# A merge whose gates take seven products for eight, with one branch's product and the plain projection ahead of them

## Chip, cores, metric

One core of a Trainium2 chip runs the whole program as one launch. The metric is device time in microseconds. The engines are TensorE (PE; its weight loads are PEld), VectorE (DVE), ScalarE (ACT), GpSimd (POOL) and SyncE (SP), which here issues loads. Each has its own queue of instructions and works through it in order.

## The reference, cut to the stretch that matters

One block over 512 rows of width 1024, in fp32. `h` is the normalised input; `w_in` projects it to eight vectors of 1024 (u, v, four for the HGRN branch, and two gates).

```python
h = _layer_norm(x, ln0_g, ln0_b)
u_r, v_r, q_r, f_r, i_r, g_r, ga_r, gb_r = split(h @ w_in + b_in)
vn  = _layer_norm(gelu(v_r), gm_norm_g, gm_norm_b)       # per 128-row block and 128-column group:
y_a = gelu(u_r) * (einsum("gts,bnsgc->bntgc", w, vn) + b_s)
y_b = _hgrn2(q_r, f_r, i_r, g_r, lb, hg_norm_g)
merged = sigmoid(ga_r) * (y_a @ w_a) + sigmoid(gb_r) * (y_b @ w_b)
h1  = _layer_norm(ALPHA * h + merged @ w_o, ln1_g, ln1_b)
hid = silu(h1 @ w_ffn_gate) * (h1 @ w_ffn_up)
out = _layer_norm(ALPHA * h1 + hid @ w_ffn_down + ple, ln2_g, ln2_b)
```

## The kernel before

**Products.** Every operand of a large product is split into a high part of a type that TensorE takes at full rate (fp32r) and a low part, the remainder; a product is three matmuls, high by high, high by low, low by high. `split` (lines 62 to 66) makes the parts: a cast on ScalarE and a subtraction on VectorE. A unit of weights of 128x1024 is loaded by SyncE into one of three "raw" buffers and split into one of five pairs `wh`, `wl`. `gemm_a` (line 85) multiplies a stripe of 256 columns of a weight by all 512 rows: two units, 48 matmuls with 512 columns. `gemm_b` has the rows as the stationary operand.

**Seven for eight.** `strassen` (line 164) forms a product of a 2x2 block matrix of weights and a 2x2 block matrix of activations with seven block products in place of eight. Its order is X Z Y Z2 Y2 W Y3; GpSimd makes two of the sums of weights and two more are transfers that add. `product_a` (line 216) is one block product: 24 matmuls with 256 columns. X, W and Y3 read the blocks "11", "12" and "22" of the activations, the others combinations of them (s1, a6, a7, a3). Before, only the FFN's gate and up have this form: eleven groups (`up`), of which each makes 256 columns of both.

**Order of the stretch.** The HGRN branch goes over four pairs of heads; the last pair's `scores`, `outputs` and `finish` are woven into the projection of v (two halves, lines 717 to 728). `finish(M)` transposes the heads, gates them and splits them into `ybh`, `ybl`, w_b's operand. Then: the norm of v (`norm_v`, four row blocks, each with VectorE, ScalarE and GpSimd, "spread"); u's four products, each with its GELU; behind each of them `mix`, which multiplies the normed v by the 128x128 matrices of w_s, adds b_s, multiplies by u and splits to `yah`, `yal`. The merge follows, four rounds over 256 output columns: gate a, w_a, gate b, w_b, 48 matmuls each, with Sigmoid on ScalarE, two multiplies and an addition on VectorE, and a split. `residual` loads x anew and norms it (ScalarE, then two GpSimd operations). Then w_o, the norm, the PLE gate, and the FFN.

**What sets the order.** Each instruction is written for one engine. A planner takes them in program order as priorities (`high_priority` moves some up), estimates their times, gives each engine a fixed order and places the buffers; a pool that has been closed gives its space to later ones, which wait for the last reader. PSUM has four tiles of two banks each.

Of the kernel before, what the change touches and what calls it, by code (L numbers as in the profile page):

```python
# [14 lines left out]
P = 128  # L15
# [18 lines left out]
def block_kernel(  # L34
# [50 lines left out]
    def gemm_a(ps, w, c0, acth, actl, name):  # L85

        for kh in range(2):
            h, l = unit_a(w, 4 * kh, c0, f"{name}_{kh}")
            for j in range(2):
                cs = slice(j * P, (j + 1) * P)  # L90
                for k in range(4):
                    kk = 4 * kh + k
                    first, last = kk == 0, kk == KT - 1
                    PE.matmul(ps[:, j, :], h[:, k, cs], acth[:, kk, :], start=first, stop=False)  # L94
                    PE.matmul(ps[:, j, :], h[:, k, cs], actl[:, kk, :], start=False, stop=False)  # L95
                    PE.matmul(ps[:, j, :], l[:, k, cs], acth[:, kk, :], start=False, stop=last)  # L96
# [621 lines left out]
    for c in range(2):  # L718
# [5 lines left out]
        for a in range(2):  # L724
# [15 lines left out]
    norm_v(3)  # L740
    hgb_cm.__exit__(None, None, None)

    rpool = ctx.enter_context(tc.tile_pool(name="rpool", bufs=1, side="right"))
    r1 = rpool.tile([P, TT, D], F32, name="r1")
    yapool_cm = tc.tile_pool(name="yapool", bufs=1, side="right")
    yapool = yapool_cm.__enter__()
    yah = yapool.tile([P, NH, T], F32R, name="yah")
    yal = yapool.tile([P, NH, T], F32R, name="yal")
    with tc.tile_pool(name="gm", bufs=1, side="right") as gp:
        bs = load_bc(gp, gm_b_s[0].rearrange("g t -> (g t)"), "bs")  # L750
        def mix(m, ug):
# [6 lines left out]
            mx = gp.tile([P, 2, T], F32, tag="mx", name=f"mx{m}", bufs=2)  # L758
            for a in range(2):
                g = 2 * m + a  # L760
                V.tensor_tensor(out=mx[:, a, :].rearrange("p (n t) -> p n t", t=P),
                                in0=psm[:, a, :].rearrange("p (n t) -> p n t", t=P),
                                in1=bs[:, g * P:(g + 1) * P].unsqueeze(1).broadcast_to([P, TT, P]), op=ALU.add)
            V.tensor_tensor(out=mx, in0=mx, in1=ug, op=ALU.mult)
            split(yah[:, 2 * m:2 * m + 2, :], yal[:, 2 * m:2 * m + 2, :], mx)

        prev = None
        for m in range(NH // 2):
            psu = proj(OU, m, "gu") if m else psu0
            ug = gp.tile([P, 2, T], F32, tag="ug", name=f"ug{m}", bufs=2)  # L770
# [11 lines left out]
    mgh = mgpool.tile([P, KT, T], F32R, name="mgh")  # L782
    mgl = mgpool.tile([P, KT, T], F32R, name="mgl")
    with tc.tile_pool(name="mg", bufs=1) as mp:

        g0a = load_bc(mp, ln0_g, "g0a")
        b0a = load_bc(mp, ln0_b, "b0a")
        S.activation(g0a, g0a, AF.Copy, scale=ALPHA)
        S.activation(b0a, b0a, AF.Copy, scale=ALPHA)
        nmr = mp.tile([P, TT, 1], F32, name="nmr")  # L790
        V.scalar_tensor_tensor(out=nmr, in0=mr0[:, :, 0:1], scalar=-1.0, in1=mr0[:, :, 1:2], op0=ALU.mult, op1=ALU.mult)

        def residual(t):
            r = r1[:, t, :]
            nc.sync.dma_start(r, xv[:, t, :])
            S.activation(r, r, AF.Identity, scale=mr0[:, t, 1:2], bias=nmr[:, t, :])
            G.tensor_tensor(out=r, in0=r, in1=g0a, op=ALU.mult)
            G.tensor_tensor(out=r, in0=r, in1=b0a, op=ALU.add)

        for m in range(KT // 2):  # L800
            residual(m)
            res = []
            for nm, off, w, ah, al in (("a", OGA, wa, yah, yal), ("b", OGB, wb, ybh, ybl)):
                psg = ps_tile(f"ps_mg{nm}{m}")
                gemm_a(psg, win, off + 256 * m, hh, hl, f"g{nm}{m}")
                sg = mp.tile([P, 2, T], F32, tag="sg", name=f"sg{nm}{m}", bufs=3)
                for a in range(2):
                    S.activation(sg[:, a, :], psg[:, a, :], AF.Sigmoid, bias=bcol(off, 2 * m + a))
                psw = ps_tile(f"ps_mw{nm}{m}")
                gemm_a(psw, w, 256 * m, ah, al, f"w{nm}{m}")  # L810
                V.tensor_tensor(out=sg, in0=psw, in1=sg, op=ALU.mult)
                res.append(sg)
            V.tensor_tensor(out=res[0], in0=res[0], in1=res[1], op=ALU.add)
            split(mgh[:, 2 * m:2 * m + 2, :], mgl[:, 2 * m:2 * m + 2, :], res[0])
    ybpool_cm.__exit__(None, None, None)
    hpool_cm.__exit__(None, None, None)
# [8 lines left out]
    with tc.tile_pool(name="l1", bufs=1) as lp:  # L825
# [229 lines left out]
```

## Time and profile before

| | before |
|---|---|
| median of 3 runs | 953.31 us (951.9 to 953.61) |
| profiled execution | 952.23 us, its span 950.5 us |
| TensorE busy in the span | 936.2 us (98%), 5552 matmuls |
| VectorE, ScalarE, GpSimd busy | 62%, 39%, 21% |
| TensorE clock granted | 0.997 on the mean of the span |

A line of the page's groups reads: line, engine, operation, tiles out<-in, shapes, count | busy time, mean ns of one | idle time of the engine before it and what ended most of it. In the timeline a row has its start in the span, its duration, engine, line, operation and tiles. Matmuls overlap: their spacing is read from starts, not from durations.

### The profile page before, as it was taken

The numbers are of one execution on the slowest core, as the hardware profiler recorded it, in microseconds if no ns is written. First come the engines' busy times: TensorE is split into PE (matmuls) and PEld (weight loads), VectorE is DVE, ScalarE is ACT, GpSimd is POOL, SyncE is SP. The second block draws the span as 40 slices with busy tenths as digits, with TensorE's granted clock in tenths as the row PEclk, the third lists the DMA queues.
The fourth block names the chain that finished last, engine by engine and source line by source line (L and its number), as shares of the span: only waits on it lengthen the run. The fifth ranks groups of instructions, "written<-read, shape, count | busy, mean of one in ns | idle before, by whom it ended". The sixth has DMA issues, their size and how long they took to land.

```text
span 950.5 us, 13396 instructions
## 1 busy us (share of the span) xinstructions
PE 936.2 (98%) x5552; PEld 811.2 (85%) x5552; DVE 587.0 (62%) x652; ACT 366.7 (39%) x456; POOL 200.1 (21%) x142
## 2 busy tenths in 40 slices
PE   8999999999999999999999999999999999999996
PEld 6888888888888888888888888899999999988885
DVE  6567944868249655423333278488878888567527
ACT  6544232333334362223222177444444445333211
POOL 2015310505006037000000001444333440000004
PEclk9999999999999999999999999999999999999998
DMA  7543223223322624232224312965676564258302
GB/s 262 172 144 111 68 69 110 67 68 110 120 81 67 222 89 133 89 103 96 89 98 169 111 70 89 267 151 146 167 168 183 137 161 106 88 190 272 114 24 88
DMA packets 85452, 120.46 MB, mean 127 GB/s; under 512 B 3992, under 2 KB 60944, under 8 KB 85392
## 3 DMA queue, kind: packets, MB, share of 16 engines
q1 hardware_dynamic: 80928, 105.93, 34.1%
q0 software_dynamic: 3168, 11.54, 7.2%
q10 hardware_dynamic: 1296, 2.15, 0.6%
q8 instruction: 43, 0.70, 0.3%
q14 instruction: 17, 0.14, 0.0%
HBM read 101.77 MB, written 6.29 MB: 114 GB/s over the span
## 4 chain that ended last, share of the span: by engine, by line
PE 90%; DVE 5%; ACT 1%; POOL 1%; issue 1%; DMA 1%; SPq 0%; DVEq 0%; POOLq 0%; ACTq 0%
PE ps_f_b L228 4%; PE ps_f_b L226 4%; PE ps_f_b L229 4%; PE ps_d L100 4%; PE ps_d L101 4%; PE ps_d L102 4%; PE ps_f_a L229 3%; PE ps_f_a L226 3%; PE ps_f_a L228 3%; PE ps_mwa L95 2%; PE ps_mwa L96 2%; PE ps_mwa L94 2%; PE ps_i L102 2%; PE ps_i L100 2%; PE ps_v L100 2%; PE ps_f L94 2%
## 5 line engine op out<-in xcount | busy, mean ns | idle before, releaser
L253 POOL TENSOR_TENSOR mr<-mr,nhalf 128x1 f32<-128x1 f32 x12 | 9.8, 821 | 335.2 <-DVE mr L252 335.2
L63 ACT CAST wh_f<-raw_f 128x1024 fp32r<-128x1024 f32 x41 | 43.2, 1053 | 86.4 <-PE ps_f_b L228 38.5
L102 PE MATMUL ps_d<-wh_d,hidl 128*128 128x512 f32 x172 | 66.8, 389 | 0.0
L101 PE MATMUL ps_d<-wl_d,hidh 128*128 128x512 f32 x172 | 66.8, 389 | 0.0
L100 PE MATMUL ps_d<-wh_d,hidh 128*128 128x512 f32 x172 | 66.0, 389 | 0.0
L66 DVE TENSOR_TENSOR wl_f<-raw_f,wh_f 128x1024 fp32r<-128x1024 f32 x41 | 51.2, 1248 | 21.4 <-ACT wh_f L63 21.3
L66 DVE TENSOR_TENSOR wl_f_t<-t_f,wh_f_t 128x1024 fp32r<-128x1024 f32 x22 | 55.5, 2521 | 3.2 <-ACT wh_f_t L63 3.0
L185 POOL TENSOR_TENSOR t_f<-raw_f,raw_f 128x1024 f32<-128x1024 f32 x11 | 26.7, 2428 | 125.9 <-DVE wl_f L66 102.3
L63 ACT CAST wh_d<-raw_d 128x1024 fp32r<-128x1024 f32 x22 | 23.1, 1050 | 62.8 <-PE ps_d L102 23.6
L501 POOL TENSOR_TENSOR k<-sgm,lv 128x512 f32<-128x512 f32 x8 | 16.0, 2023 | 121.6 <-DVE lv L553 121.6
L66 DVE TENSOR_TENSOR wl_d<-raw_d,wh_d 128x1024 fp32r<-128x1024 f32 x22 | 26.9, 1221 | 18.7 <-ACT wh_d L63 18.7
L102 PEld LDWEIGHTS ps_d<-wh_d,hidl 128*128 128x128 f32 x172 | 32.3, 188 | 6.7
L100 PEld LDWEIGHTS ps_d<-wh_d,hidh 128*128 128x128 f32 x172 | 32.2, 188 | 6.6
L101 PEld LDWEIGHTS ps_d<-wl_d,hidh 128*128 128x128 f32 x172 | 32.3, 188 | 6.5
L63 ACT CAST wh_f_t<-t_f 128x1024 fp32r<-128x1024 f32 x22 | 23.1, 1051 | 32.8 <-PE ps_f_b L229 18.0
L185 POOL TENSOR_TENSOR t_f<-t_f,raw_f 128x1024 f32<-128x1024 f32 x11 | 35.1, 3189 | 0.9
L66 DVE TENSOR_TENSOR wl_wb<-raw_wb,wh_wb 128x1024 fp32r<-128x1024 f32 x8 | 14.2, 1779 | 25.7 <-ACT wh_wb L63 25.7
L66 DVE TENSOR_TENSOR wl_wa<-raw_wa,wh_wa 128x1024 fp32r<-128x1024 f32 x8 | 9.8, 1225 | 27.7 <-ACT wh_wa L63 27.7
L66 DVE TENSOR_TENSOR wl_wo<-raw_wo,wh_wo 128x1024 fp32r<-128x1024 f32 x8 | 9.8, 1222 | 25.8 <-ACT wh_wo L63 25.8
L940 DVE TENSOR_TENSOR g<-p,ps_f_b 128x512 f32<-128x512 f32 x11 | 7.6, 688 | 28.8 <-PE ps_f_b L229 28.7
L94 PE MATMUL ps_q<-hh,wh_q 128*128 128x512 f32 x64 | 25.2, 394 | 0.0
L94 PE MATMUL ps_mwa<-yah,wh_wa 128*128 128x512 f32 x64 | 25.2, 394 | 0.0
(376 smaller groups left out, 3186.0 us busy)
## 6 DMA issues: line engine op xcount, KB each, us to landing
raw_f<-in_w_ffn_up_dram SPq DMA_DIRECT2D x22, 512.0 KB, 7.6
raw_f<-in_w_ffn_gate_dram SPq DMA_DIRECT2D x22, 512.0 KB, 3.6
raw_d<-in_w_ffn_down_dram SPq DMA_DIRECT2D x22, 512.0 KB, 3.7
raw_f<-raw_f POOLq DMA_DIRECT2D x11, 512.0 KB, 4.9
t_f<-raw_f POOLq DMA_DIRECT2D x11, 512.0 KB, 7.2
raw_i<-in_w_in_dram SPq DMA_DIRECT2D x8, 512.0 KB, 4.3
raw_f<-in_w_in_dram SPq DMA_DIRECT2D x8, 512.0 KB, 3.7
raw_q<-in_w_in_dram SPq DMA_DIRECT2D x8, 512.0 KB, 3.7
```

Of the source, the lines that this page charges most:

```text
L63: S.copy(h, src)
L66: (eng or V).tensor_tensor(out=l, in0=src, in1=h.bitcast(F32), op=ALU.subtract)
L94: PE.matmul(ps[:, j, :], h[:, k, cs], acth[:, kk, :], start=first, stop=False)
L95: PE.matmul(ps[:, j, :], h[:, k, cs], actl[:, kk, :], start=False, stop=False)
L96: PE.matmul(ps[:, j, :], l[:, k, cs], acth[:, kk, :], start=False, stop=last)
L100: PE.matmul(ps, acth[:, kk, ts], h[:, k, :], start=first, stop=False)
L101: PE.matmul(ps, acth[:, kk, ts], l[:, k, :], start=False, stop=False)
L102: PE.matmul(ps, actl[:, kk, ts], h[:, k, :], start=False, stop=last)
L185: G.tensor_tensor(out=d, in0=a, in1=b, op=ALU.add)
L226: PE.matmul(o, h[:, k, cs], ah[:, k, :], start=first and j == 0 and k == 0, stop=False, skip_group_check=True)
L228: PE.matmul(o, h[:, k, cs], al[:, k, :], start=False, stop=False, skip_group_check=True)
L229: PE.matmul(o, l[:, k, cs], ah[:, k, :], start=False, stop=last and j == 1 and k == 3, skip_group_check=True)
```

## The change

- **Order.** After v come `finish(M)`, the norm of v, w_b's four products with a copy of each result to `mgf` in SBUF (ScalarE), the mix of all eight groups behind w_b's second and third product (result and b_s to `yaf`), u's four products (GELU, multiplied into `yaf`), the gates, w_a's four products.
- **Gates.** `group_a` is the FFN's group, taken out of `up` with its evacuation as a parameter. Four groups make 256 columns of both gates each. Sigmoid is applied in halves with the bias; gate a is stored to DRAM (issued from ScalarE) and loaded again in w_a's stage, gate b is multiplied into `mgf`. The blocks "11", "12" and "22" of h are read in place; `combine_h` makes the four combinations within u's first two products (four GpSimd sums of 128x512 a half, subtractions and splits).
- **y_a** is split in two halves, one within the first gate group, one after the last group in space that h held.
- **Norms.** The norm of v and the residual use `normed(..., False)`: two scalar_tensor_tensors on VectorE in place of a spread over three engines. The residuals of two row blocks go into w_a's stage and two into w_o's. r1 takes the buffer of `yaf`.
- **Merge's results** are split into four pairs of tiles (`mgs`), where there was one pair.

```diff
+    def gemm_t(ps, w, c0, act, name):      # gemm_a with the operand given by a function
...
-    def norm_v(t):
+    finish(M)
+    for t in range(TT):
         mr = gv.tile([P, 2], F32, tag="mrv", name=f"mrv{t}", bufs=2)
-        ln_stats(gv, [vn[:, t, 0:512], vn[:, t, 512:1024]], mr, f"v{t}")
-        normed(vn[:, t, :], mr, gmg, gmb, True)
-
-    norm_v(0)
-    psu0 = proj(OU, 0, "gu")
-    norm_v(1)
-    finish(M)
-    norm_v(2)
-    norm_v(3)
+        ln_stats(gvv, [vn[:, t, 0:512], vn[:, t, 512:1024]], mr, f"v{t}")
+        normed(vn[:, t, :], mr, gmg, gmb, False)
...
+        for m in range(KT // 2):
+            psw = ps_tile(f"ps_mwb{m}")
+            gemm_a(psw, wb, 256 * m, ybh, ybl, f"wb{m}")
+            S.copy(mgf[:, 2 * m:2 * m + 2, :], psw)
+            if m == 1:
+                mix(0)
+                mix(1)
+            elif m == 2:
+                mix(2)
+                mix(3)
...
+        def combine_h(i):
+            f = {}
+            for n, ks, t0 in (("21", 0, HT), ("22", 4, HT), ("11", 0, 0), ("12", 4, 0)):
+                at = (slice(None), slice(ks, ks + 4), slice(t0 + i * P, t0 + i * P + P))
+                f[n] = gp.tile([P, 4, P], F32, tag=f"f{n}", name=f"f{n}_{i}")
+                G.tensor_tensor(out=f[n], in0=hh[at].bitcast(F32), in1=hl[at].bitcast(F32), op=ALU.add)
+            f["s1"] = gp.tile([P, 4, P], F32, tag="fs1", name=f"fs1_{i}")
+            lo = slice(i * P, i * P + P)
+            for n, o, x, y in (("s1", "s1", "21", "22"), ("a7", "21", "21", "11"), ("a6", "11", "11", "s1"), ("a3", "12", "12", "11")):
+                V.tensor_tensor(out=f[o], in0=f[x], in1=f[y], op=ALU.subtract)
+                split(hcomb[n][0][:, :, lo], hcomb[n][1][:, :, lo], f[o])
+
+        for m in range(KT // 2):
+            psu = ps_tile(f"ps_u{m}")
+            gemm_a(psu, win, OU + 256 * m, hh, hl, f"u{m}")
+            if m < 2:
+                combine_h(m)
+            ug = up_.tile([P, 2, T], F32, tag="ug", name=f"ug{m}", bufs=2)
             for a in range(2):
                 S.activation(ug[:, a, :], psu[:, a, :], AF.Gelu_apprx_tanh, bias=bcol(OU, 2 * m + a))
+            y = yaf[:, 2 * m:2 * m + 2, :]
+            V.tensor_tensor(out=y, in0=y, in1=ug, op=ALU.mult)
+    with tc.tile_pool(name="gt", bufs=1) as fp:
+        def out_g(m):
+            def out(i, j, o):
+                for a in range(2):
+                    S.activation(o[:, a, :], o[:, a, :], AF.Sigmoid, bias=bcol((OGA, OGB)[j], 2 * m + a))
+                if j == 0:
+                    S.dma_start(ga_dram[:, 2 * m:2 * m + 2, HT * i:HT * i + HT], o)
+                else:
+                    y = mgf[:, 2 * m:2 * m + 2, HT * i:HT * i + HT]
+                    V.tensor_tensor(out=y, in0=y, in1=o, op=ALU.mult)
+            return out
+
+        for m in range(KT // 2):
+            group_a(wx, fp, [(win, OGA + 256 * m), (win, OGB + 256 * m)], hcomb, f"g{m}", out_g(m))
+            if m == 0:
+                split_ya(yas_pool, 0)
...
     with tc.tile_pool(name="mg", bufs=1) as mp:
+        split_ya(mp, 1)
...
         def residual(t):
-            r = r1[:, t, :]
-            nc.sync.dma_start(r, xv[:, t, :])
-            S.activation(r, r, AF.Identity, scale=mr0[:, t, 1:2], bias=nmr[:, t, :])
-            G.tensor_tensor(out=r, in0=r, in1=g0a, op=ALU.mult)
-            G.tensor_tensor(out=r, in0=r, in1=b0a, op=ALU.add)
+            nc.sync.dma_start(r1[:, t, :], xv[:, t, :])
+            normed(r1[:, t, :], mr0[:, t, :], g0a, b0a, False)
 
         for m in range(KT // 2):
-            residual(m)
...
+            ga = mp.tile([P, 2, T], F32, tag="ga", name=f"ga{m}", bufs=2)
+            nc.sync.dma_start(ga, ga_dram[:, 2 * m:2 * m + 2, :])
+            psw = ps_tile(f"ps_mwa{m}")
+            gemm_t(psw, wa, 256 * m, lambda kk: tuple(z[:, kk % 4, :] for z in yas[kk // 4]), f"wa{m}")
+            if m in (1, 2):
+                residual(m - 1)
+            with tc.high_priority(offset=400):
+                V.tensor_tensor(out=ga, in0=psw, in1=ga, op=ALU.mult)
+            o = mgf[:, 2 * m:2 * m + 2, :]
+            V.tensor_tensor(out=o, in0=o, in1=ga, op=ALU.add)
+            mgs.append(tuple(mgpool.tile([P, 2, T], F32R, name=f"mg{z}{m}") for z in "hl"))
+            split(*mgs[m], o)
```

## Rows read from the trace of the kernel before

**Rows 1.** The page's busy times by engine: us (share of the span) xinstructions.

```profile
PE 936.2 (98%) x5552; PEld 811.2 (85%) x5552; DVE 587.0 (62%) x652; ACT 366.7 (39%) x456; POOL 200.1 (21%) x142
```

**Rows 2.** The chain that ended last, share of the span by engine.

```profile
PE 90%; DVE 5%; ACT 1%; POOL 1%; issue 1%; DMA 1%; SPq 0%; DVEq 0%; POOLq 0%; ACTq 0%
```

**Rows 3.** TensorE's waits, first and last of five: us in total, times, longest.

```profile
PE ps_x L365 <- DVE mr L252: 2.5, 1, 2.5
...
PE ps_vec L386 <- DMA vec<-in_ln_b_dram: 0.4, 1, 0.4
```

**Rows 4.** Timeline of TensorE, merge: first matmul of products, and w_o's first.

```profile
340.80 0.48 PE L94 MATMUL ps_mga<-hh,wh_ga 128*128 128x512 f32 x1
...
351.77 0.39 PE L94 MATMUL ps_mwa<-yah,wh_wa 128*128 128x512 f32 x1
...
362.98 0.39 PE L94 MATMUL ps_mgb<-hh,wh_gb 128*128 128x512 f32 x1
...
516.33 0.39 PE L100 MATMUL ps_wo<-wh_wo,mgh 128*128 128x512 f32 x1
```

**Rows 5.** Timeline of TensorE, FFN's groups: first matmul of products.

```profile
683.49 0.28 PE L226 MATMUL ps_f_b<-c12h,wh_f 128*128 128x256 f32 x1
...
686.37 0.29 PE L226 MATMUL ps_f_b<-ca6h,wh_f_t 128*128 128x256 f32 x1
...
689.45 0.28 PE L226 MATMUL ps_f_b<-c22h,wh_f_t 128*128 128x256 f32 x1
...
692.17 0.28 PE L229 MATMUL ps_f_a<-cs1h,wl_f_t 128*128 128x256 f32 x1
...
780.83 0.28 PE L226 MATMUL ps_f_b<-c12h,wh_f 128*128 128x256 f32 x1
```

**Rows 6.** Stretch: us, PE PEld DVE ACT POOL busy, clock, DMA; merge twice, FFN.

```profile
340.80:384.75 43.95, 43.95 (x195) 36.09 (x194) 24.28 (x15) 19.50 (x21) 24.98 (x8) 1.00 0.38 119
384.75:428.62 43.87, 43.87 (x194) 36.01 (x193) 14.42 (x12) 11.80 (x14) 0.00 (x0) 1.00 0.30 96
...
671.00:690.40 19.40, 19.40 (x170) 19.40 (x169) 16.36 (x15) 8.90 (x10) 7.36 (x4) 1.00 0.66 163
```

**Rows 7.** Timeline of TensorE: u's first product, and the last heads' transposes.

```profile
289.30 0.39 PE L94 MATMUL ps_gu<-hh,wh_gu 128*128 128x512 f32 x1
...
300.18 1.04 PE L668 MATMUL ps_t<-ident,on 128*128 128x128 f32 x8
```

**Rows 8.** Timeline of VectorE around the norm of v.

```profile
289.13 1.29 DVE L259 BATCH_NORM_STATS2 lnst_v<-vn 128x6 f32<-128x512 f32 x2 [1.12 <-ACT vn L728]
...
292.79 1.27 DVE L268 SCALAR_TENSOR_TENSOR vn<-vn,mrv,gmg 128x1024 f32<-128x1024 f32 x1
...
301.81 3.22 DVE L268 SCALAR_TENSOR_TENSOR vn<-vn,mrv,gmg 128x1024 f32<-128x1024 f32 x1
304.95 1.40 DVE L671 SCALAR_TENSOR_TENSOR gt<-ps_t,vecT,gt 128x512 f32<-128x512 f32 x2
...
308.82 3.41 DVE L66 TENSOR_TENSOR ybl<-gt,ybh 128x1024 fp32r<-128x1024 f32 x1
```

**Rows 9.** The page's costliest groups: casts, subtractions, GpSimd's sums.

```profile
L185 POOL TENSOR_TENSOR t_f<-raw_f,raw_f 128x1024 f32<-128x1024 f32 x11 | 26.7, 2428 | 125.9 <-DVE wl_f L66 102.3
L63 ACT CAST wh_d<-raw_d 128x1024 fp32r<-128x1024 f32 x22 | 23.1, 1050 | 62.8 <-PE ps_d L102 23.6
L501 POOL TENSOR_TENSOR k<-sgm,lv 128x512 f32<-128x512 f32 x8 | 16.0, 2023 | 121.6 <-DVE lv L553 121.6
L66 DVE TENSOR_TENSOR wl_d<-raw_d,wh_d 128x1024 fp32r<-128x1024 f32 x22 | 26.9, 1221 | 18.7 <-ACT wh_d L63 18.7
...
L185 POOL TENSOR_TENSOR t_f<-t_f,raw_f 128x1024 f32<-128x1024 f32 x11 | 35.1, 3189 | 0.9
```

**Rows 10.** Timeline of GpSimd in the norm of v.

```profile
301.54 2.40 POOL L271 TENSOR_TENSOR vn<-vn,gmb 128x1024 f32<-128x1024 f32 x1
```

**Rows 11.** Timeline of ScalarE: Sigmoid of a gate before.

```profile
354.16 1.27 ACT L808 ACTIVATE sga<-ps_mga,vecT 128x512 f32<-128x512 f32 x2
```

More of the change, by code (lines that the diff above doesn't have):

```diff
@@ L93, in gemm_a @@
                     first, last = kk == 0, kk == KT - 1
-                    PE.matmul(ps[:, j, :], h[:, k, cs], acth[:, kk, :], start=first, stop=False)
-                    PE.matmul(ps[:, j, :], h[:, k, cs], actl[:, kk, :], start=False, stop=False)
-                    PE.matmul(ps[:, j, :], l[:, k, cs], acth[:, kk, :], start=False, stop=last)
+                    ah, al = act(kk)
+                    PE.matmul(ps[:, j, :], h[:, k, cs], ah, start=first, stop=False)
+                    PE.matmul(ps[:, j, :], h[:, k, cs], al, start=False, stop=False)
+                    PE.matmul(ps[:, j, :], l[:, k, cs], ah, start=False, stop=last)
     def mm_b(ps, t, acth, actl, kk, h, l, k, first, last):
@@ L765, in mix @@
[L765 to L770, printed above, removed]
+        for m in range(KT // 2):
[8 more added lines that the diff above has]
+                mix(3)
@@ new lines, in block_kernel, with group_a, prod, new @@
+    gmv_cm.__exit__(None, None, None)
+    ybpool_cm.__exit__(None, None, None)
+    def group_a(wx, fp, srcs, comb, name, out):
+        psa, psb = ps_tile(f"ps_{name}_a"), ps_tile(f"ps_{name}_b")
+        bank = {"X": psa[:, 0, :], "Z": psa[:, 1, :], "Y": psb[:, 0, :], "W": psb[:, 1, :]}
+        v = {n: b.rearrange("p (a c) -> p a c", c=HT) for n, b in bank.items()}
+        t = {}
+        def prod(chain, units, n, first, last):
+            product_a(bank[chain], units, comb[n], first, last)
+        def new(n, bufs=1):
+            t[n] = fp.tile([P, 2, HT], F32, tag=n, name=f"{n}_{name}", bufs=bufs)
+            return t[n]
+        def evac(n):
+            if n == "p1":
+                S.copy(new("p1", 2), v["X"])
+            elif n in ("y6", "z5"):
+                V.tensor_tensor(out=new(n), in0=v[n[0].upper()], in1=t["p1"], op=ALU.subtract)
+            else:
+                i, j = int(n[1]) - 1, int(n[2]) - 1
+                x, y, op = {"c11": (v["W"], "p1", ALU.add), "c22": (v["Y"], "z5", ALU.add),
+                            "c12": (v["Z"], "y6", ALU.add), "c21": (v["Y"], "p1", ALU.subtract)}[n]
+                o = new(f"{'gu'[j]}{i}")
+                if n == "c21":
+                    V.tensor_tensor(out=o, in0=t[y], in1=x, op=op)
+                else:
+                    V.tensor_tensor(out=o, in0=x, in1=t[y], op=op)
+                out(i, j, o)
+        strassen(wx, [[src_a(w, 4 * a, c0) for w, c0 in srcs] for a in range(2)], name,
+                 "X Z Y Z2 Y2 W Y3", prod, evac)
@@ new lines, in block_kernel, with split_ya @@
+    yas = []
+    def split_ya(pool, k):
+        h = pool.tile([P, 4, T], F32R, name=f"yah{k}")
+        l = pool.tile([P, 4, T], F32R, name=f"yal{k}")
+        for i in range(2):
+            split(h[:, 2 * i:2 * i + 2, :], l[:, 2 * i:2 * i + 2, :], yaf[:, 4 * k + 2 * i:4 * k + 2 * i + 2, :])
+        yas.append((h, l))
+    yas_cm = tc.tile_pool(name="yas", bufs=1, side="right")
+    yas_pool = yas_cm.__enter__()
+    hcpool_cm = tc.tile_pool(name="hcpool", bufs=1, side="right")
+    hcpool = hcpool_cm.__enter__()
@@ L800, in block_kernel @@
-        for m in range(KT // 2):
-            residual(m)
[L802 to L814, printed above, removed]
```

99 lines of the change are left out of this document (41 added, 58 removed).

## The prediction

> **What bounds the kernel now.** I read the page's busy times first, then the chain that ended last, then the waits of TensorE, and last the timeline of the stretch that the change rewrites. TensorE is busy for 98% of the span, and VectorE, the next engine, for 62% [rows 1]. The chain of waits runs through TensorE for 90% of the span [rows 2]. TensorE's own waits are five entries of 6.2 us together, from 2.5 us for the first norm's statistics down to 0.4 [rows 3]; the others are for the opening's zeros, for the heads' outputs and for the PLE gate's operand, none for an operand of the merge. So the time is the sum of matmul issue intervals, and a change is worth what it takes out of that sum, less any wait that it opens.
>
> In the old merge a product of 48 matmuls of 512 columns runs from one first matmul to the next in 10.97 us (first gate product of a round), and w_a's in 11.21 us; the four rounds take 516.33 - 340.80 = 175.53 us [rows 4]. Without w_a's four this leaves 130.7 us for twelve products, 10.89 us each, or 227 ns a matmul. The granted clock is 1.00 there, the 2.4 GHz level [rows 6].
>
> The kernel already has the form that the gates are to take: the FFN's gate and up, seven products of 24 matmuls with 256 columns a pair of column blocks. The product on "12" starts at 683.49 in one group and at 780.83 five groups later: 19.47 us a group [rows 5]. In a group TensorE is busy throughout, VectorE for 16.4 of 19.4 us, ScalarE for 8.9, GpSimd for 7.4 [rows 6]. Not all products cost the same: the one on "22" takes 692.17 - 689.45 = 2.72 us (113 ns a matmul), the one on "12" 686.37 - 683.49 = 2.88 us (120 ns) [rows 5].
>
> **The change part by part.**
>
> Gates. Eight products of 48 matmuls go: one at 10.97 and seven at 10.89, 87.2 us [rows 4]. Four groups of 168 matmuls come, at the FFN group's 19.47 us: 77.9 us [rows 5]. That is **-9.3 us**. Bounds: every matmul at the fast 113.3 ns makes a group 19.03 us and the gain 11.1; every one at the slow 120 ns makes it 20.16 us and the gain 6.6. I take the FFN's mean, since the order of the products and the ratio of operands read in place ("11", "12", "22") to combined ones is the same.
>
> What a group feeds on. Against the FFN's group the evacuation is the same (one copy, six VectorE operations, two multiplies); Sigmoid runs in halves with a bias, eight ScalarE instructions in place of two. Even at 0.64 us each, what one of 512 columns takes [rows 11], that is 5.1 us on an engine with 8.9 of 19.4 busy. Two stores to DRAM per group are issued from ScalarE. Group 0 also splits half of y_a, two casts and two subtractions of 128x1024 at 1.05 and 1.22 us [rows 9], 2.4 us on VectorE's 3.0 us of slack. All of it is hidden by TensorE's 19.47 us: nothing added.
>
> w_b, u and w_a. Their products keep 48 matmuls each, so moving them costs nothing. One number may move: w_a's products run 0.32 us longer than the others [rows 4], for a reason that the trace doesn't show; with y_a in other buffers they may run at 227 ns (-1.3 us over four) or w_b's may go at 233 (+1.3). I take nothing.
>
> Seam v to w_b. Before, u's first product (10.9 us, 289.30 to 300.18) stood between v and the last heads' transposes [rows 7]. That cover is gone: w_b needs those heads. After the transposes (0.8 us) VectorE makes gt (1.40 us for two), ScalarE casts (1.05), VectorE subtracts (1.22) [rows 8, 9]; with one evacuation of v ahead (1.2) and signalling, about 5.3 us after v's end. w_b touches heads 6 and 7 only with its 31st matmul, 0.8 + 30 x 0.227 = 7.6 us after v's end: hidden with 2.3 us to spare. The other bound: before, this chain took from 300.18 to 312.2, because it stood in VectorE's queue behind the norm of v and ran beside GpSimd [rows 7, 8]; put that way again, w_b would wait 4.4 us. In program order it now stands ahead of the norm, so I take nothing.
>
> Norm of v on VectorE alone. A row block has statistics (1.29 us), small operations (some 0.3) and now two scalar_tensor_tensors (1.2 to 1.27 each) [rows 8]: about 4.05 us, four blocks 16.2 us. With the last evacuation, the heads' 2.6 us and four weight subtractions of w_b (4.9 us), VectorE has 24.9 us from 289.1, so it ends at 314. The mix wants all four blocks when two w_b products are done, at 289.3 + 0.8 + 21.8 = 311.9. Two us late if the mix is ahead of w_b's third product in TensorE's order, nothing if a half product of w_b goes first. I take **+1.0 us**, between 0 and 3. What helps: GpSimd's adds disappear. Beside one, a scalar_tensor_tensor took 3.22 us in place of 1.27 [rows 8, 10].
>
> Combinations of h in the u stage. GpSimd gets eight sums of 128x512 (2.02 us) and the first group's two of 128x1024 (2.43 and 3.19) [rows 9]: 21.8 us. VectorE gets eight weight subtractions (9.8), sixteen operations of 512 columns (half of 1.22 and a little, 0.65: 10.4), four multiplies (4.9) and three subtractions for group 0 (3.7): 28.8 us. Beside GpSimd it goes at some 0.4 of its rate (1.27 to 3.22), so 21.8 us of overlap gets 8.7 us of that done and the rest takes 20.1: 41.9 us in a stage of 43.9. Just hidden by u's matmuls; the sums can also begin while w_b's last product runs. Nothing added, up to +3 if the order is bad.
>
> Gates to w_a. The second half of y_a's split goes into space that the last gate product still reads (h), so it starts only when that ends: c21's evacuation (0.7), two casts and two subtractions in pairs, ready about 4.2 us later; w_a reads it with matmul 25, 5.45 us later. Hidden by 1.2 us; two weight splits ahead in the queue would make it +1.2. The reload of the stored gate waits for the same moment on SyncE's queue, and w_a's weights queue behind it; the next are due 10.9 us later and need about 6 (landing, cast, subtraction), so it is hidden unless the first two are behind it too: then +6. I take nothing, since two of five weight buffers stand free for them during the last group.
>
> Residual. Four blocks of two VectorE operations, 10 us in w_a's and w_o's stretches, where VectorE was busy for 14.4 of 43.9 us a round [rows 6]: hidden. The 25 us of GpSimd that go, all in the first round [rows 6], were hidden too: that round took no longer than the others but for 0.1 us.
>
> Sum: -9.3 + 1.0 = **-8.3 us**. The profiled execution took 952.23 us with a span of 950.5; the median of the runs is 953.31, 1.1 above it. On the median that is **945.0 us**.
>
> The rows give a 256-column matmul just half of the interval of a 512-column one (113 to 120 ns against 227) [rows 4, 5]. The Trainium skill, "TensorE: Matmul & The Clock Gate", section Back-to-back issue gap, says otherwise for a stream in which each matmul loads its weights: about 81 ns at 128 columns and 131 at 512. On a line between these, an estimate from that page, 256 columns take 98 ns, so a group takes 16.4 us against 12.6 for two plain products, and the change loses 15 us over four groups. The trace speaks against it, both in the interval at 512 and in the ratio.
>
> **The rivals.**
> (a) VectorE paces the gate groups. For it: 16.4 of 19.4 us busy, and group 0 has 2.4 more [rows 6]. Against: the FFN's eleven groups run without a TensorE wait on the same load. The gain is gone when a group takes 21.8 us, 5.4 us more VectorE work than the row shows; then 952 to 954 us. Chance 0.05, with stalls at the seams that sum to about 8 us.
> (b) Slower: VectorE and GpSimd collide in the u stage. If GpSimd's sums run as slowly as the contended rows and VectorE with them, the stage's 41.9 us grow, by 0.6 us for each us more of GpSimd; the first group waits for its combinations and u's later weights come late. It decides from 10 us of stall, which is 17 us of GpSimd beyond 21.8; with 15 us of stall 960 us. Against: only 22 us of sums are there. Chance 0.06.
> (c) Slower: matmuls of 256 columns cost more than half. The point is 87.2 / 672 = 130 ns. If the issue intervals stood to each other as the rows' durations do, 0.28 to 0.39 us [rows 4, 5], they would be 163 ns and the gates 109.5 us, 22 us more: 975 us. All eleven FFN groups are against it [rows 5]. Chance 0.02.
> The rule of the Trainium skill above is of this kind.
> (d) Forecast's kind: TensorE stays full and the gates gain 6.6 to 11.1 us, less up to 6 at the seams: 941 to 951 us. Chance 0.87.
>
> **How the numbers follow.** The forecast is (d)'s 945.0. Its lower end is all matmuls fast and w_a at 227 ns (-12.4): 941. Its upper end is all slow (-6.6) with 4 us at the seams: 950.5. What lies beyond is 0.13 from (a) to (c) and a little of (d). A measurement of this kernel tells about 0.2%, 1.9 us, from no change: faster (below 951.4) 0.87, within 0.05, slower 0.08.
>
> **What the profile of the changed kernel would show.** Right: gate groups 19.0 to 20.2 us apart with TensorE busy throughout; w_b's first product directly behind the transposes, no wait of TensorE above 3 us at the mix, at the first group's second product, or at matmul 25 of w_a; scalar_tensor_tensors of the norm at 1.2 to 1.3 us. Wrong: groups near 22 us with TensorE waiting for a subtraction of weights; waits on ybl, on vn, on the combinations or on y_a's second half; a granted clock below 1.00 after such a wait.

## The result and the profile after

The changed kernel takes 944.4 us (median) against 952.82 for the kernel before on the same chip: ratio 0.9913, 95% interval [0.9901, 0.9924]. The profiled execution took 943.88 us with a span of 942.2, before 952.23 and 950.5. The forecast was 945.0, in 941.0 to 950.5. The medians here leave out two executions of the experiments' kernels, of 1550 and 1879 us, that took far longer than the others.

The page's busy times of the changed kernel answer to [rows 1]; below them its chain of waits by engine, which answers to [rows 2].

```profile
PE 926.5 (98%) x5840; PEld 817.2 (87%) x5840; DVE 639.5 (68%) x719; ACT 384.2 (41%) x492; POOL 207.0 (22%) x154
...
PE 88%; DVE 6%; ACT 2%; POOL 2%; issue 1%; DMA 1%; SPq 0%; DVEq 0%; ACTq 0%; POOLq 0%
```

TensorE issues 288 matmuls more (672 of 256 columns in place of 384 of 512) and is busy for 9.7 us less. VectorE took up 52.5 us of work and stands at 68%.

TensorE's waits in the changed kernel, all six, answer to [rows 3]. Columns: us in total, times, longest.

```profile
PE ps_x L369 <- ACT wh_ple L63: 1.6, 1, 1.6
PE ps_warm L322 <- POOL wz L317: 1.5, 1, 1.5
PE ps_t L672 <- DVE on L663: 1.5, 3, 0.7
PE ps_g_b L230 <- DVE u_g L807: 1.2, 1, 1.2
PE ps_vec L390 <- DMA vec<-in_ln_b_dram: 1.1, 1, 1.1
PE ps_pg L106 <- DVE c11l L66: 0.5, 1, 0.5
```

One of them is new and lies in the stretch that was rewritten: 1.2 us in the gates, for `u_g`. There is none at the mix, none at w_b, none at w_a.

Timeline of TensorE in the changed kernel, the first matmul of each stage (transposes, w_b, mix, u, gates), the first behind the last gate product, and w_o's first; it answers to [rows 4] and [rows 7].

```profile
288.72 1.03 PE L672 MATMUL ps_t<-ident,on 128*128 128x128 f32 x8
289.51 0.47 PE L98 MATMUL ps_mwb<-ybh,wh_wb 128*128 128x512 f32 x1
...
311.37 0.38 PE L758 MATMUL ps_mx<-wsT,vn 128*128 128x128 f32 x2
...
340.38 0.39 PE L98 MATMUL ps_u<-hh,wh_u 128*128 128x512 f32 x1
...
383.90 0.28 PE L230 MATMUL ps_g_a<-hh,wh_g 128*128 128x256 f32 x1
...
474.49 0.40 PE L100 MATMUL ps_mwa<-yah,wl_wa 128*128 128x512 f32 x1
...
507.76 0.39 PE L104 MATMUL ps_wo<-wh_wo,mgh 128*128 128x512 f32 x1
```

From v's end to w_o's first matmul it is 507.76 - 288.72 = 219.04 us, before 516.33 - 289.30 = 227.03 [rows 4, 7]: -8.0 us. What comes ahead of v's end is 0.6 us shorter, what follows w_o's first matmul 0.3 us longer. Summed from the starts of the products in both traces, the 8.0 us are: gates 87.22 to 79.63 (-7.6), w_a 44.80 to 44.23 (-0.6), u 43.82 to 43.52 (-0.3), w_b 43.50 to 44.06 (+0.6), mix and transposes -0.1. The last gate group stands woven with w_a, whose first matmul runs at 455.06; each product counts where it runs.

Stretches of the changed kernel: w_b's first two products, u, three successive stretches of the gates (each about one group long, since neighbouring groups overlap), w_a's end. They answer to [rows 6]: us, then PE PEld DVE ACT POOL busy, granted clock, DMA share, GB/s.

```profile
289.51:311.37 21.86, 21.86 (x99) 18.12 (x98) 21.01 (x29) 6.71 (x8) 5.76 (x4) 1.00 0.34 103
...
340.38:383.90 43.52, 43.52 (x193) 36.04 (x192) 29.61 (x24) 17.04 (x21) 18.57 (x10) 1.00 0.67 181
383.90:403.42 19.52, 19.52 (x170) 19.51 (x169) 15.18 (x14) 11.81 (x15) 6.83 (x4) 1.00 0.36 98
403.42:423.00 19.58, 18.40 (x159) 18.20 (x158) 16.21 (x15) 11.16 (x17) 7.21 (x5) 1.00 0.72 188
423.00:442.50 19.50, 19.50 (x169) 19.50 (x169) 13.72 (x17) 11.40 (x18) 1.58 (x2) 1.00 0.45 120
474.49:507.76 33.27, 33.27 (x147) 27.22 (x146) 28.09 (x25) 11.13 (x12) 0.00 (x0) 1.00 0.66 231
```

The reader is to see that TensorE is full in every stretch but the fourth line's, which lacks 1.18 us, and that VectorE is tightest ahead of the mix: 21.0 of 21.9 us.

The one new wait, in three engines' timelines of the changed kernel (start, duration, then in brackets the idle time before and its releaser):

```profile
421.40 0.39 PE L230 MATMUL ps_g_b<-hh,wh_g 128*128 128x256 f32 x1 [1.18 <-DVE u_g L807]
...
415.70 2.23 DVE L66 TENSOR_TENSOR wl_g_t<-t_g,wh_g_t 128x1024 fp32r<-128x1024 f32 x1 [0.34 <-ACT wh_g_t L63]
417.86 2.88 DVE L865 TENSOR_TENSOR mgf<-mgf,u_g 128x512 f32<-128x512 f32 x1
420.67 0.68 DVE L807 TENSOR_TENSOR u_g<-ps_g_b,z_g 128x512 f32<-128x512 f32 x1
...
416.93 3.26 POOL L189 TENSOR_TENSOR t_g<-t_g,raw_g 128x1024 f32<-128x1024 f32 x1
```

The product on "12" needs the PSUM tile that the evacuation of block c22 of the result into `u_g` empties; that evacuation starts at 420.67. That operation stands in VectorE's queue behind the multiply by gate b. Alone the multiply takes 0.68 us (at 422.40); beside GpSimd's sum of weights, from 416.93 to 420.19, it took 2.88 and ended 0.55 us after that sum. This is the collision of [rows 8, 10] at a new place.

### The profile page after: what moved, and what is told of

Its sections match the earlier page's. It is cut to its first block, busy times and chain, and to the rows that moved or that the text cites. A ratio compares the mean times of both kernels' runs of the same rounds, so it can differ in the third digit from the quotient of the medians.

```text
span 942.2 us, 14188 instructions
## 1 busy us (share of the span) xinstructions
PE 926.5 (98%) x5840; PEld 817.2 (87%) x5840; DVE 639.5 (68%) x719; ACT 384.2 (41%) x492; POOL 207.0 (22%) x154
## 4 chain that ended last, share of the span: by engine, by line
PE 88%; DVE 6%; ACT 2%; POOL 2%; issue 1%; DMA 1%; SPq 0%; DVEq 0%; ACTq 0%; POOLq 0%
PE ps_f_b L230 4%; PE ps_f_b L232 4%; PE ps_f_b L233 4%; PE ps_d L106 4%; PE ps_d L104 4%; PE ps_d L105 4%; PE ps_f_a L233 3%; PE ps_f_a L230 3%; PE ps_f_a L232 3%; PE ps_i L106 2%; PE ps_mwa L98 2%; PE ps_i L104 2%; PE ps_mwa L99 2%; PE ps_v L104 2%; PE ps_f L98 2%; PE ps_mwa L100 2%
## 5 line engine op out<-in xcount | busy, mean ns | idle before, releaser
L66 DVE TENSOR_TENSOR wl_f<-raw_f,wh_f 128x1024 fp32r<-128x1024 f32 x41 | 51.2, 1249 | 22.0 <-ACT wh_f L63 21.9
L66 DVE TENSOR_TENSOR wl_d<-raw_d,wh_d 128x1024 fp32r<-128x1024 f32 x22 | 26.8, 1220 | 18.7 <-ACT wh_d L63 18.6
L66 DVE TENSOR_TENSOR wl_g<-raw_g,wh_g 128x1024 fp32r<-128x1024 f32 x20 | 25.3, 1264 | 20.6 <-ACT wh_g L63 20.6
L63 ACT CAST wh_g<-raw_g 128x1024 fp32r<-128x1024 f32 x20 | 21.0, 1051 | 43.1 <-PE ps_f L99 10.9
L805 DVE TENSOR_TENSOR g_f<-p_f,ps_f_b 128x512 f32<-128x512 f32 x11 | 7.6, 688 | 28.8 <-PE ps_f_b L233 28.8
L98 PE MATMUL ps_g<-hh,wh_g 128*128 128x512 f32 x64 | 25.2, 394 | 0.0
L98 PE MATMUL ps_mwb<-ybh,wh_wb 128*128 128x512 f32 x64 | 25.2, 393 | 0.0
```

The source lines that it names most:

```text
L63: S.copy(h, src)
L66: (eng or V).tensor_tensor(out=l, in0=src, in1=h.bitcast(F32), op=ALU.subtract)
L98: PE.matmul(ps[:, j, :], h[:, k, cs], ah, start=first, stop=False)
```

## The experiments

**Only the order, only the gates: `plain_gates`.** The changed order, with the eight plain products put back.

```diff
-            if m < 2:
-                combine_h(m)
...
-            group_a(wx, fp, [(win, OGA + 256 * m), (win, OGB + 256 * m)], hcomb, f"g{m}", out_g(m))
+            for j, off in enumerate((OGA, OGB)):
+                psg = ps_tile(f"ps_g{j}{m}")
+                gemm_a(psg, win, off + 256 * m, hh, hl, f"g{j}{m}")
...
```

> The new order with the gates as eight plain products of 48 matmuls, without the combinations of h. My theory, the gates' products give all of it: gates 87.2 us in place of the 79.6 that four groups took, so 7.0 to 8.0 us slower than the changed kernel, 951.5 to 952.5 us, no different from the kernel before within 0.2%. Rival, the order and the lighter GpSimd give some of it: it stays 2 us or more below the kernel before (below 950.8). Rival, the order costs and the groups give more than that: it is above the kernel before by 2 us.

Measured 952.31 us, ratio to before 0.9998 [0.9989, 1.0007]. Timeline of TensorE, first gate product and first of w_a:

```profile
384.48 0.39 PE L98 MATMUL ps_g<-hh,wh_g 128*128 128x512 f32 x1
...
471.52 0.39 PE L98 MATMUL ps_mwa<-yah,wh_wa 128*128 128x512 f32 x1
```

87.04 us for 384 matmuls, 227 ns each, as before. The new order with everything else is worth nothing that the medians can tell; the whole gain comes with the seven products. In this trace v's end to w_o's first matmul is 226.46 us, 0.6 less than before, as much as w_a's products lost (44.24 for 44.80). Whether the seven products would gain as much in the old order, no run here shows.

**Only the norms: `norms_alone`.** The kernel before with the norm of v and the residual on VectorE.

```diff
-        normed(vn[:, t, :], mr, gmg, gmb, True)
+        normed(vn[:, t, :], mr, gmg, gmb, False)
...
-            G.tensor_tensor(out=r, in0=r, in1=g0a, op=ALU.mult)
-            G.tensor_tensor(out=r, in0=r, in1=b0a, op=ALU.add)
+            normed(r, mr0[:, t, :], g0a, b0a, False)
```

> The kernel before with only the norm of v and the residual on VectorE alone, order and gates as before. My theory, both are hidden behind TensorE's matmuls: within 1 us of the kernel before. Rival, GpSimd's additions slowed VectorE where TensorE waited: 1 to 3 us faster, with the operations on ybl and the weights at 1.2 us in place of 2 to 3.4. Rival, VectorE's queue gets too long ahead of the mix: 1 to 3 us slower, with a wait of TensorE at the mix.

Measured 953.18 us, ratio 1.0004 [0.9995, 1.0013]: hidden in the old order, as in the prediction.

**The norms back in the new order: `spread_back`.** The changed kernel with both norms spread again.

```diff
-        normed(vn[:, t, :], mr, gmg, gmb, False)
+        normed(vn[:, t, :], mr, gmg, gmb, True)
...
-            normed(r1[:, t, :], mr0[:, t, :], g0a, b0a, False)
+            normed(r1[:, t, :], mr0[:, t, :], g0a, b0a, True)
```

> The changed kernel with the norm of v and the residual spread again over ScalarE and GpSimd, as in the kernel before; all else as in the changed kernel. Theory: a norm that has w_b's first two products in front of it (21 us) has room either way, so the time stays at 944.4, within 943 to 946; TensorE has no wait at the mix. Rival: GpSimd's additions run beside VectorE's scalar_tensor_tensors again and stretch them from 1.27 to about 3.2 us, the heads' low part and the norm come late, and TensorE waits between v and the mix; with four stretched ones, 4 x 2 us, and the thin cover that the prediction gave the heads, the time is 948 to 952.

Measured 946.13 us, ratio to before 0.9927 [0.9911, 0.9944], which overlaps the changed kernel's. The trace tells more than the time. TensorE, GpSimd and VectorE at the mix:

```profile
315.49 2.50 PE L758 MATMUL ps_mx<-wsT,vn 128*128 128x128 f32 x20 [1.14 <-POOL vn L275]
...
309.13 6.31 POOL L275 TENSOR_TENSOR vn<-vn,gmb 128x1024 f32<-128x1024 f32 x2
...
304.07 3.38 DVE L272 SCALAR_TENSOR_TENSOR vn<-vn,mrv,gmg 128x1024 f32<-128x1024 f32 x1
```

The norm ends at 315.4 instead of 310.5 (309.25 + 1.27 in the changed kernel), TensorE waits for it, and from v's end to u it is 53.04 us instead of 51.66. So the theory of this run fell: TensorE waits at the mix, as its rival said, but for 1.4 us in all and not 4 to 8. Of the norm's scalar_tensor_tensors one was stretched (3.38 us) and not four. What came last were GpSimd's last two additions, 6.31 us together from 309.13, where VectorE's own operation takes 1.27 each. Nothing of it came from the heads.

**Program order of the heads: `heads_last`.** `finish(M)` behind the norm's loop instead of ahead of it.

```diff
-    finish(M)
     for t in range(TT):
...
+    finish(M)
```

> The changed kernel with the last heads' finish behind the norm of v in program order. My forecast held that the cover of the seam from v to w_b is thin and that the order ahead of the norm pays for it: w_b should wait 2 to 5 us for the heads' low part, 1 to 5 us slower than the changed kernel. Rival, TensorE has other work there or the norm leaves gaps enough: no wait, 0 us.

Measured 944.82 us, ratio 0.9913 [0.99, 0.9927], and no wait at w_b. The planner gave VectorE the same order (the gating of the heads at 290.94, their subtraction at 295.87), so this run does not price the cover that the prediction gave the heads.

**The wait in the gates: `late_multiply` and `one_multiply`.** First, both multiplies by gate b written behind the second evacuation:

```diff
+            late = []
...
-                else:
+                    return
+                late.append((i, o))
+                for i, o in late if len(late) == 2 else ():
                     y = mgf[:, 2 * m:2 * m + 2, HT * i:HT * i + HT]
```

> The changed kernel with both multiplies of gate b into the stored product behind the second one's evacuation. In the changed kernel TensorE waits 1.2 us in the second gate group for c22's evacuation, and a multiply of 2.88 us stands ahead of that in VectorE's queue. My theory, that multiply is the cause: the wait goes, 1.0 to 1.5 us faster. Rival, the evacuation is late because of the weight subtraction or the cast ahead of it: the wait stays or moves to another group, 0 us.

Measured 944.57 us, ratio 0.9918 [0.9905, 0.9932]. VectorE's timeline shows why it tells nothing: the planner kept the queue as it was.

```profile
419.99 2.89 DVE L869 TENSOR_TENSOR mgf<-mgf,u_g 128x512 f32<-128x512 f32 x1
422.80 0.68 DVE L807 TENSOR_TENSOR u_g<-ps_g_b,z_g 128x512 f32<-128x512 f32 x1
```

So, second, both halves of gate b in one tile and one multiply of 1024 columns, which can't run before the second evacuation:

```diff
+            both = fp.tile([P, 2, T], F32, tag="both", name=f"both{m}")
+
+            def place(i, j):
+                return both[:, :, HT * i:HT * i + HT] if j else None
...
-                else:
-                    y = mgf[:, 2 * m:2 * m + 2, HT * i:HT * i + HT]
-                    V.tensor_tensor(out=y, in0=y, in1=o, op=ALU.mult)
+                elif i == 1:
+                    y = mgf[:, 2 * m:2 * m + 2, :]
+                    V.tensor_tensor(out=y, in0=y, in1=both, op=ALU.mult)
```

> The changed kernel with gate b's two halves in one tile and one multiply of 1024 columns into the stored product after both, so that the first multiply can't stand ahead of c22's evacuation in VectorE's queue. My theory, it was what delayed the evacuation: TensorE's wait of 1.2 us in the second gate group goes, 1.0 to 1.5 us faster than the changed kernel. Rival, weight subtractions slowed by GpSimd's sums delay it: the wait stays at 0.5 us or more, there or in another group.

VectorE's timeline there:

```profile
416.32 2.07 DVE L66 TENSOR_TENSOR wl_g_t<-t_g,wh_g_t 128x1024 fp32r<-128x1024 f32 x1 [0.34 <-ACT wh_g_t L63]
418.34 0.69 DVE L807 TENSOR_TENSOR both<-ps_g_b,z_g 128x512 f32<-128x512 f32 x1
419.37 2.37 DVE L66 TENSOR_TENSOR wl_g_t<-t_g,wh_g_t 128x1024 fp32r<-128x1024 f32 x1 [0.34 <-ACT wh_g_t L63]
421.66 1.21 DVE L870 TENSOR_TENSOR mgf<-mgf,both 128x1024 f32<-128x1024 f32 x1
```

The evacuation follows the subtraction directly, TensorE's waits have no entry for the gates any more, and the four groups take 78.31 us instead of 79.63. The cause of the wait is thus shown, and its price: 1.3 us in the trace, where v's end to w_o's first matmul is 217.71 us in place of 219.04. By the clock it is 944.55 us, ratio 0.9908 [0.9895, 0.9922]: the span of its trace is 941.6 against 942.2, and by the median it can't be told from the changed kernel. The start of the program varies by more: in kernels that do the same up to there, v's end lies between 288.50 (`sums_twice`) and 290.84 us (`late_multiply`).

**GpSimd in u's stage: `sums_thrice` and `sums_twice`.** Each of the eight sums of `combine_h` three times, then twice.

```diff
-                G.tensor_tensor(out=f[n], in0=hh[at].bitcast(F32), in1=hl[at].bitcast(F32), op=ALU.add)
+                for _ in range(3):
+                    G.tensor_tensor(out=f[n], in0=hh[at].bitcast(F32), in1=hl[at].bitcast(F32), op=ALU.add)
```

> The changed kernel with each of the eight GpSimd sums that make the combinations of h done three times instead of once: 16 more sums of 1.5 to 1.7 us, about 26 us of GpSimd more in the stage of u. The result is the same numbers. Rival (b) of the prediction: VectorE is slowed by 0.6 us for each us of GpSimd, the stage has 2 us to spare, so from 26 us more TensorE waits some 12 to 14 us in u's products or ahead of the first gate group: 956 to 959. Theory: the sums start within w_b's last product and VectorE is busy for 29.6 of u's 43.5 us, 14 us free, so that the stage takes most of it: 944 to 947, with a TensorE wait of 0 to 2 us.

Measured 952.4 us, ratio 0.9994 [0.9984, 1.0003]: the whole gain gone. TensorE's timeline behind u in this run, and two rows of VectorE's and ScalarE's:

```profile
391.28 0.39 PE L230 MATMUL ps_g_b<-ha6h,wh_g_t 128*128 128x256 f32 x1 [2.41 <-ACT wh_g_t L63]
...
393.69 0.39 PE L233 MATMUL ps_g_b<-ha6h,wl_g_t 128*128 128x256 f32 x1 [1.91 <-DVE wl_g_t L66]
...
398.92 0.39 PE L230 MATMUL ps_g_a<-hs1h,wh_g_t 128*128 128x256 f32 x1 [0.84 <-ACT p_g L796]
...
386.13 2.89 DVE L66 TENSOR_TENSOR ha6l<-f,ha6h 128x512 fp32r<-128x512 f32 x1
...
389.66 0.62 ACT L63 CAST ha3h<-f 128x512 fp32r<-128x512 f32 x1 [4.22 <-DVE f L844]
```

The stage of u in this run, and a stretch behind the waits, with the columns of the stretches above:

```profile
342.31:385.83 43.52, 43.52 (x193) 36.05 (x192) 41.06 (x22) 15.48 (x20) 36.23 (x21) 1.00 0.44 133
...
394.20:397.30 3.10, 3.10 (x16) 3.10 (x16) 3.10 (x4) 2.17 (x4) 0.60 (x1) 0.50 0.90 208
```

u's own products lose nothing (43.52 us). VectorE is busy for 41.1 of these 43.5 us and is late with the last combinations of h. ScalarE's cast for a3 waits for it until 389.66, and behind that cast stands the cast of a sum of gate weights, which the second product (on a6) reads: TensorE waits 2.4 us for it and 1.9 for VectorE's subtraction, then 0.8 ahead of the third product. After the first two waits the granted clock falls to 0.50, the 1.2 GHz level, for about 3.2 us; the spacing is 213 ns there instead of 114, some 1.5 us more. The first two products, with the next wait, end at 398.92, 13.09 us after u, against 5.62 in the changed kernel: 7.5 us. The collision of rival (b) is real, then; both numbers on record missed its size, 0 to 2 and 12 to 14.

How the two engines collide shows at the stage's start, in the timelines of VectorE and GpSimd:

```profile
337.93 10.16 DVE L66 TENSOR_TENSOR wl_u<-raw_u,wh_u 128x1024 fp32r<-128x1024 f32 x1 [5.03 <-ACT wh_u L63]
...
331.71 15.30 POOL L840 TENSOR_TENSOR f<-hh,hl 128x512 f32<-128x512 f32 x12 [22.39 <-PE ps_mx L758]
```

A subtraction that takes 1.21 us alone lasted 10.16 us. It began within an unbroken row of twelve sums and ended 1.1 us after the row did. So VectorE didn't go at a lower rate here: the operation was held until the row was over.

> The changed kernel with each of the eight GpSimd sums for the combinations of h done twice, so half as much is added as in the run with three: about 12.5 us of GpSimd. Three cost 7.6 us between u's end and the second gate product's end and put VectorE at 41.1 us busy of u's 43.5, against 29.6 in the changed kernel. Theory (room that is used up first): half of the additional 11.5 us puts VectorE at 35.3 of 43.5, the sums still end before the last u product, and TensorE waits for nothing new: 944 to 945.5, with no wait at the second gate product. Rival (every microsecond of GpSimd costs its share): half of 7.6 us is lost, 947.5 to 949, with a wait at the second gate product of 2 to 4 us.

Measured 944.88 us, ratio 0.9927 [0.9911, 0.9944]. The stretch that is nearly u's stage in the run with two sums:

```profile
342.00:385.50 43.50, 43.50 (x201) 36.33 (x200) 39.87 (x29) 20.26 (x28) 26.85 (x15) 1.00 0.56 157
```

TensorE waits for nothing new. VectorE grew more than expected (39.9 us, not 35.3) and still nothing was lost. The sums take 23.5 us in this trace, 12.6 in the changed kernel and 38.3 in the run with three. So the stage has room for at least some 11 us of GpSimd beyond what the change put there, and less than 26: a point from which it decides, not a share of each microsecond.

**Where buffers lie: `pad_left`, `pad_left64`, `pad_h1`, `memset_again`.** These ask about the other part of the gates' shortfall: products that read h in place go at 120 ns, those on combinations at 113. A pad of 32 bytes (`pad_left`, the first lines) or 64 (`pad_left64`, `[P, 16]`) moves all buffers of one side; `pad_h1`'s 64 bytes (the last lines) move, of the products' operands, only "11" and "12" of the FFN.

```diff
+    pad = const.tile([P, 8], F32, name="pad")
+    G.memset(pad, 0.0)
...
+    pad = h1pool.tile([P, 16], F32, name="pad")
+    G.memset(pad, 0.0)
```

> The changed kernel with one more tile of 32 bytes a partition in the first pool, which moves all buffers on that side by 32 bytes and changes no operation. In the gate groups matmuls of 256 columns that read h in place are 120 ns apart and those that read the combinations 113; h starts 32 bytes into a block of 256, the combinations 224. My theory, the spacing goes with the place at which an operand starts: the products on h go to 113 ns or so, 1.9 us less in the gates and 3.5 us less on the FFN's 11 and 12, so 4 to 7 us faster. Rival, it goes with the side of the memory or with the operand's stride: 0 us, both spacings stay.

> The changed kernel with 64 bytes a partition ahead of all buffers of the left side: weights, h and the FFN's 11 and 12 go to 96 bytes into a block of 128, where the combinations are already. If the place against the weights counts, all 256-column products go at 120 ns (the combinations lose 2.6 us in the gates and 8.8 in the FFN) and w_a's first halves at 227 (0.6 us back): 10 us slower than the changed kernel, near 955 us. If the moving operand's own place counts, products on h go at 113 ns with 256 columns and at 233 with 512: 5.4 us back and 6.4 lost, within 2 us of the changed kernel.

> The changed kernel with 64 bytes a partition ahead of the FFN's operands 11 and 12, and nothing else moved. They then start 96 bytes into a block of 128, as the combinations do, and the weights still at 32. My theory, what counts is the place of the moving operand against that of the weights in a block of 128 bytes: 11 and 12 go from 120 to 113 ns, 2 x 24 x 11 matmuls, 3.5 us faster than the changed kernel. Rival, it is the pool or the side of the memory: 0 us, 120 ns stay.

Measured, in this order: 951.07 us, ratio 0.9988 [0.9979, 0.9997]; 952.53 us, 0.9995 [0.9986, 1.0005]; 948.26 us, 0.9948 [0.9934, 0.9961]. Four successive product starts of the gates' first group, first in the changed kernel's timeline:

```profile
386.78 0.29 PE L230 MATMUL ps_g_b<-ha6h,wh_g_t 128*128 128x256 f32 x1
...
389.52 0.28 PE L230 MATMUL ps_g_a<-hs1h,wh_g_t 128*128 128x256 f32 x1
392.24 0.28 PE L230 MATMUL ps_g_b<-ha7h,wh_g_t 128*128 128x256 f32 x1
394.96 0.28 PE L230 MATMUL ps_g_a<-ha3h,wh_g 128*128 128x256 f32 x1
```

The same four in the timeline with the pad of 64 bytes on one side:

```profile
387.37 0.28 PE L230 MATMUL ps_g_b<-ha6h,wh_g_t 128*128 128x256 f32 x1
...
390.22 0.28 PE L230 MATMUL ps_g_a<-hs1h,wh_g_t 128*128 128x256 f32 x1
393.07 0.28 PE L230 MATMUL ps_g_b<-ha7h,wh_g_t 128*128 128x256 f32 x1
395.91 0.28 PE L230 MATMUL ps_g_a<-ha3h,wh_g 128*128 128x256 f32 x1
```

2.74, 2.72 and 2.72 us a product become 2.85, 2.85 and 2.84: 119 ns. With 2520 matmuls of 256 columns in the program, a few nanoseconds each are most of the 8 us lost. But the third run went against its theory. Its timeline in the FFN, with the products of [rows 5]:

```profile
678.26 0.28 PE L230 MATMUL ps_f_b<-c12h,wh_f 128*128 128x256 f32 x1
681.09 0.28 PE L230 MATMUL ps_f_b<-ca6h,wh_f_t 128*128 128x256 f32 x1
...
684.27 0.28 PE L230 MATMUL ps_f_b<-c22h,wh_f_t 128*128 128x256 f32 x1
687.09 0.28 PE L233 MATMUL ps_f_a<-cs1h,wl_f_t 128*128 128x256 f32 x1
```

Both products take the same now: "12" 2.83 us instead of 2.88, "22" 2.82 instead of 2.72. The pad moved two operands and slowed the FFN's others, which lay where they were, from 113 or 114 ns to 117 (a7 had 117 before), while "11" and "12" only gained 2 ns; the gates, outside the pad's reach, stayed at 113 and 120. A rule by which each operand's own place sets its speed is refuted. All three pads brought one instruction more, so a control:

```diff
     G.memset(nhalf, -0.5)
+    G.memset(nhalf, -0.5)
```

> The changed kernel with one small memset of a constant tile done twice on GpSimd at the start: no buffer moves, but there is one instruction more. It is the control for the runs with pads, which had a memset as well as a moved buffer. If the spacing of the matmuls of 256 columns follows from where buffers lie, it stays at 113 ns for the combinations and 120 for h in place, and the time is 944.4, within 943 to 946. If it follows from anything else that one more instruction changes, the spacing goes to about 118 ns throughout, 1848 + 672 matmuls by up to 4 ns, and the time is 948 to 952.

Measured 944.0 us, ratio 0.9905 [0.989, 0.992], with 113 ns on combinations as in the changed kernel. One more instruction does nothing; it is where the buffers lie. By what rule stays open.

## Why the prediction was right, point by point

The forecast sum was -8.3 us and the profiled executions differ by 943.88 - 952.23 = -8.35. The agreement is better than the terms: errors cancel, and part of that is luck.

- **Gates**, -9.3 predicted, -7.6 measured: the mis-sized term. The old side was right (87.22 for 87.2). The new side is 79.63 for 77.9. Of the 1.7 us, 1.3 are the wait for the evacuation, which `one_multiply` takes out. The step that failed there is "all of it is hidden by TensorE's 19.47 us": I costed the evacuation by busy time, and counted the two multiplies as the FFN's, but not that one of them would stand ahead of an evacuation while GpSimd sums weights. The remaining 0.4 us is in the main the block "22", which is read in place here at 119 to 120 ns and lies in a buffer of its own in the FFN at 113 to 114 [rows 5]: 96 matmuls by 5.5 ns are 0.5. The product on a7 goes the other way, 114.5 ns for 117: -0.2. So the premise that the operands stand as in the FFN held only in part.
- **Order**, nothing predicted: right for order and norms together, and shown by `plain_gates`.
- **Seam v to w_b**, nothing predicted, nothing there: w_b starts 0.79 us after the transposes begin. The cover was wider than worked out. The planner put matmuls of w_b's second product among the first's, so that the last heads' low part, ready at 297.1, is first read by about the 56th matmul, at 302.1, and not by the 32nd. How it goes with a thin cover stays open: `heads_last`, meant to thin it, left the order as it was.
- **Norm to mix**, +1.0 predicted, no wait measured. VectorE ended at 310.5 and not at 314: two of the eight half-row statistics were done before v's end, and an operation starts some 0.08 us ahead of the shown end of the one before it (one of the norm's, 1.27 us from 306.91, is followed at 308.11), which a sum of durations counts twice. What w_b gained (+0.6) isn't this term: most of it is in its second half, whose matmuls now stand among those of the mix, as u's did before (u -0.3). `spread_back` shows the other side of the term: here, unlike in the old order, the norm on VectorE alone is worth 1.4 us.
- **Seam gates to w_a**, nothing predicted, nothing there, with far more cover than the 1.2 us worked out: TensorE's order has w_a's matmuls on the first half of y_a among the last gate products, from 455.06, and the second half was split by 479.9. So the term was right for another reason than the one given.
- **w_a and the rest**, nothing predicted. w_a has -0.6: its second half runs at 227 ns and the first still at 233. Ahead of v's end it is -0.6 and behind w_o's start +0.3. What lies ahead of v's end can't be told from chance: the place of v's end varies by 2.3 us from run to run. These terms, with the norm that cost no wait, cancel the gates' shortfall.
- **GpSimd's sums**: 1.30 to 1.76 us each, not 2.02; they began at 329.79 in w_b's last product, so u's stage held 18.6 us of GpSimd and not 21.8. Of these, 6.6 are two sums for the second group (from 364.56), which the prediction didn't count.

The rivals. (a) VectorE as the pace of the gate groups: it was busy for 15.2 of 19.5 us in the first stretch and 16.2 in the second, and TensorE stayed full but for the one wait. (b) The collision in u's stage: it didn't make TensorE wait, and the runs show how far off that was, between 11 and 26 us of GpSimd. It was put at 17 us beyond 21.8 for 10 us of stall (with the 2 us that the stage had to spare, its own sum gives 20); 26 more than the change's own load gave 7.5. So the two engines do collide, but the slope was too steep and its form wrong: a rate of 0.4 doesn't describe an operation that is held through a whole row of sums. (c) 256 columns at over half: refuted by 113 to 120 ns. The rule of the Trainium skill beside it ("TensorE: Matmul & The Clock Gate", Back-to-back issue gap: 81 ns sustained at 128 columns, 131 at 512) is not borne out here: products of 512 columns ran at 227 to 233 ns. The same section's figures for an isolated matmul, 262 cycles at 256 columns and 518 at 512, make 109 and 216 ns at 2.4 GHz, an estimate from that page that stands much nearer to the 113 to 120 and 227 to 233 measured; by its ratio the change gains, as it did.

## What to carry to other kernels

Where TensorE is full, seven products for eight are worth their matmuls: price them by spacing between starts of the same form elsewhere in the trace, not by a busy time. Then look, at each place where an evacuation frees PSUM, for what stands ahead of it on its engine, and at what speed that goes beside GpSimd; a busy share with 3 us of room in 19 did not exclude a wait of 1.2. An edit off the critical path (here, a norm on one engine instead of three) can be worth nothing in one order and 1.4 us in another.

## What the hardware showed that was not expected

- The spacing of matmuls of 256 columns has levels near 113, 117 and 119 to 120 ns at a granted clock of 1.00, and a pad of 32 or 64 bytes that shifts the buffers of one side moved products from one to another: 944.4 us became 951.1 and 952.5, nearly as much as the whole change brought. The rule was not found.
- A VectorE operation on two SBUF operands that begins beside a GpSimd sum took up to some four times as long as alone: 2.88 against 0.68 us for 512 columns, and 3.38 against 1.27 for a scalar_tensor_tensor of 1024. Beside an unbroken row of sums it was held until the row's end: 10.16 us in `sums_thrice` and 5.07 in `sums_twice`, against 1.21. Operations with one operand in PSUM kept their time beside such sums: 0.69 us at 414.68 in the changed kernel.
- Two waits of TensorE, 2.4 and 1.9 us with two matmuls between them, were followed by 3.1 us at a granted clock of 0.50; a single wait of 1.2 us in the changed kernel was not (1.00 behind it). At the lower level the spacing at 256 columns was 213 ns.
